# The first unit of an up projection made as plain products, with a written order for VectorE and ACT around it

## The chip, the cores and the metric

One core of one Trainium2 chip runs the whole block. The metric is the device time of one execution in microseconds (us), the median of repeated runs. The engines are TensorE (PE: matmuls, and PEld, its weight loads), VectorE (DVE), ScalarE (ACT), GpSimd (POOL) and SyncE (SP), which here issues the transfers between memory and the on-chip arrays. TensorE accumulates in banks of PSUM; all else lies in SBUF.

## What is computed

A decoder block on 1024 tokens of width 1024, in float32:

```python
h = rms_norm(x, mix_norm_g)
proj = h @ w_in
...
x = x + merged @ w_out
h2 = rms_norm(x, ffn_norm_g)
up = h2 @ w_up                      # 1024 x 5632
a, val = up[..., :D_FF], up[..., D_FF:]      # D_FF = 2816
a = causal_depthwise_conv(a, conv_w, conv_b) # 3 taps over tokens
x = x + (gelu(a) * val) @ w_down
return rms_norm(x, final_norm_g)
```

The case is about the end of `merged @ w_out` and the start of `h2 @ w_up`.

## The kernel before

**Arithmetic.** Each float32 operand of a matmul is split in a high part (a rounded copy, made on ACT, L161) and a low part (the rest, a subtraction, L162, on VectorE or POOL); this is `to_parts`. A product of two operands takes three matmuls, high·high, high·low and low·high (`PASSES`).

**Products.** Large products are made by a scheme of seven products in place of eight (Strassen-Winograd). The left matrix is quartered (A11, A12, A21, A22; first index the half of the tokens, second the half of the inner dimension), and the seven products P1 to P7 take as left operands A11, A12, A22 and the sums S1, S2, S3, S4; the right operands are sums of quarters of the weights. A product of the up projection has 4 steps of the inner dimension with 3 matmuls each: 12 matmuls of a 128x128 weight with 512 tokens. P2 is added into the PSUM bank of P1, P4 into that of P7, P3 into that of P5, so a product that reopens a bank must wait until the bank's first content has been read out.

**Up projection.** 22 units. Unit `ff` is 128 columns of the gate and 128 columns of the value, for both halves of the tokens (four results of 128x512). `up_op` (with `weight_op`, L253 to L276) makes the weight operands, `up_product` issues the matmuls (L1566) and what reads their banks: P1's bank is copied by ACT (`t1`, L1579), after P2 it is the gate of the first half of the tokens, which goes through `convolve` (an Identity with bias on ACT, L1523, two shifted multiply-adds on VectorE, L1525, with the two columns at the edge of the halves kept in `edge`, then a Gelu on ACT, L1532); `u2 = t1 + P6`, `v = u2 + P7` (L1587), and so on to the second gate `c21` and the two values; POOL multiplies gates and values (L1595, L1599); SP stores them in DRAM (`gd`). The list `order` sets in which order PE takes the products: the first two units, and P1 and P2 of the third, are interleaved, then each unit takes P1 and P2 of the next between its own products. `up_ahead` issues loads of weights up to nine places, operands up to four places ahead. P1's and P2's operands lie in rows 12 to 15 of the array `R`, the others in a pool of four buffers. For unit 0 VectorE stands in for POOL (`free`).

**Left operands.** `left_parts` splits a left matrix into 4 high and 4 low parts of 128x512. Rows of arrays are fixed (A11, A12 in `G0`, A22, S2 in `G1`, S3, S1, S4 in `R`).

**Output projection.** Its seven products run in the order P1, P2, P6, P5, P3, P7, P4 (L1454), each over four blocks of 128 tokens and four steps. When P3 (blocks 0 to 3) or P4 (blocks 4 to 7) of a block is read out (L1447), the block is complete: ACT squares it (`square_h`, L1411), POOL makes the scale (`finish_rms`, L1788 to L1793), ACT and VectorE scale one half each (`xn`, L1420 and L1421), PE transposes it (`turn_h`, `ht`, L1368), VectorE multiplies the gain in (L1372), and for the blocks 4 to 7 `sums` (L215 to L220) makes the sources of S1 to S4 out of two blocks. `after` and `tick` put a step a few matmuls further on.

**Order.** PE runs in the order of the program. The order of VectorE, ACT and POOL is set by a scheduler that places each instruction by its own estimates; each engine then works its list strictly in order and waits where an input or a buffer is not there yet.

Of the kernel before, what the change touches and what calls it, by code (L numbers as in the profile page):

```python
# [11 lines left out]
F32 = mybir.dt.float32  # L12
# [8 lines left out]
P = 128  # L21
# [72 lines left out]
def block_kernel(  # L94
# [115 lines left out]

    def sums(rows_of, raw, s3, b, eng):

        a11, a12 = raw[:, b - 4, lower], raw[:, b - 4, upper]
        a21, a22 = raw[:, b, lower], raw[:, b, upper]
        eng.tensor_tensor(s3[:, b - 4, :], a11, a21, ALU.subtract)  # L215
        nc.vector.tensor_tensor(a21, a21, a22, ALU.add)  # L216
        nc.vector.tensor_tensor(a11, a21, a11, ALU.subtract)
        if b == NB - 1:
            left_parts(rows_of, "S2", raw[:, 0:4], 0)
        nc.vector.tensor_tensor(a12, a12, a11, ALU.subtract)  # L220
# [1037 lines left out]
    def out_op(s):  # L1258

        if s < 3:  # L1260
            t = two(lead, s)
        elif (s - 3) % 8 < 4:
            t = two(R, 12 + (s - 3) % 8)
        else:
            t = wq.tile([P, 2, HALF], F32R, name=f"op_wo_{s}", tag="op", bufs=4)
# [43 lines left out]
    UP_ROWS = MIX_ROWS  # L1309
# [15 lines left out]

    def up_op(ff, name):
        if name in ("P1", "P2"):
            counts["up_op"] += 1
            row = 12 + counts["up_op"] % 4
            op = R[:, row, :].rearrange("p (a k c) -> p a k c", a=2, k=QK)  # L1330
        else:
            op = wq.tile([P, 2, QK, P], F32R, name=f"op_{name}_{ff}", tag="op", bufs=4)
        free = nc.vector if ff == 0 else nc.gpsimd
# [17 lines left out]
    def up_ahead(i, far, look):  # L1351

        while ready["load"] < min(i + far, len(order)):
# [4 lines left out]
        while ready["op"] < min(i + look, len(order)):  # L1358
            up_op(*order[ready["op"]])
            ready["op"] += 1  # L1360

    GAIN = 8 + NCT + 4 * NFF

    def turn_h(b, xn):
        for c in range(2):
            pt = (acc_tile if out_raw else tr_tile)(f"ht_{b}_{c}")
# [14 lines left out]
        if b >= 4:  # L1381
            sums(UP_ROWS, Y, s3, b, nc.vector)

# [31 lines left out]
    def finish_h(b):  # L1415

        nc.sync.dma_start(x1_t[:, b, :], Y[:, b, :])
        rs = finish_rms(nc, small, mhalf, sqs2[b], f"n2_{b}")
        xn = [temp(f"xn_{b}_{c}") for c in range(2)]
# [513 lines left out]
```

## Time and profile before

| | us |
|---|---|
| median of 3 runs | 1430.82 (1429.61 to 1431.01) |
| profiled execution | 1429.11 |
| its span | 1427.4 |
| PE busy in the span | 1388.0 (97%) |
| VectorE / ACT / POOL busy | 1016.4 / 650.6 / 313.7 |

The times of single instructions are from the profiled execution, counted from the start of its span. The difference of 1.7 us between the profiled execution's time and its span lies around the span. An instruction's row has its start, its duration, engine, line, the result and the operands, and in brackets how long the engine had been idle ahead of it and what it waited for.

### The profile page before, as it was taken

To read this page: it belongs to the slowest core of one execution; us is meant where nothing else is said; L and a number is where in the kernel's file an instruction comes from. 1 tells how busy PE (TensorE), PEld (TensorE's weight loads), DVE (VectorE), ACT (ScalarE), POOL (GpSimd) and SP (SyncE) were. 2 spreads that over 40 slices of the span, in tenths; PEclk is the share of its full clock that TensorE was granted. 3 is DMA by queue.
4 is the path that set the end of the run, shared out by engine and by line. 5 is a ranking of instruction groups with operands and counts; after the bars stand their busy time and mean duration, and the time that the engine had idled before them with its cause. 6 is when DMAs were issued, how large, how long until landed. Compare 5 with 4: busy or idle time off the path is not lost. (4 is left out here: it accounts for less than half of the span.)

```text
span 1427.4 us, 19350 instructions
## 1 busy us (share of the span) xinstructions
PE 1388.0 (97%) x6522; PEld 1145.4 (80%) x6522; DVE 1016.4 (71%) x1888; ACT 650.6 (46%) x1266; POOL 313.7 (22%) x303
## 2 busy tenths in 40 slices
PE   8899999999999999999998799999999999999997
PEld 7777788888888788887886588888888887888886
DVE  7877677676886987768878866665666557676674
ACT  5554255555553333534455433433333435354453
POOL 0002000000231000111001555556655544000002
PEclk9999999999999999999999999999999999999999
DMA  6013635354435996793731222223333226987663
GB/s 238 15 49 104 193 88 182 97 171 134 137 113 189 332 309 232 230 301 119 265 133 59 82 103 76 91 92 118 118 118 109 90 97 229 379 307 242 198 208 118
DMA packets 140338, 230.71 MB, mean 162 GB/s; under 512 B 13392, under 2 KB 57168, under 8 KB 140240
## 3 DMA queue, kind: packets, MB, share of 16 engines
q1 hardware_dynamic: 138800, 227.33, 47.7%
q10 hardware_dynamic: 1440, 2.16, 0.4%
q8 instruction: 51, 0.84, 0.2%
q14 instruction: 47, 0.39, 0.1%
HBM read 163.57 MB, written 64.29 MB: 160 GB/s over the span
## 5 line engine op out<-in xcount | busy, mean ns | idle before, releaser
L477 PE MATMUL in_P<-R,G 128*128 128x512 f32 x1008 | 243.8, 394 | 0.0
L477 PEld LDWEIGHTS in_P<-R,G 128*128 128x128 f32 x1008 | 185.7, 188 | 36.8
L1688 PE MATMUL dn<-R 128*128 128x512 f32 x924 | 209.6, 389 | 0.0
L1688 PEld LDWEIGHTS dn<-R 128*128 128x128 f32 x924 | 173.5, 188 | 36.0
L1566 PE MATMUL uP<-R,op_P 128*128 128x512 f32 x792 | 191.4, 395 | 0.0
L1566 PEld LDWEIGHTS uP<-R,op_P 128*128 128x128 f32 x792 | 149.6, 189 | 34.9
L161 ACT ACTIVATE G<-wr 128x512 fp32r<-128x512 f32 x126 | 79.1, 629 | 152.0 <-PE in_P L477 114.7
L1566 PE MATMUL uP<-G,op_P 128*128 128x512 f32 x528 | 133.2, 401 | 11.9 <-DVE Y L1587 7.8
L1566 PEld LDWEIGHTS uP<-G,op_P 128*128 128x128 f32 x528 | 100.6, 192 | 37.7 <-issue 7.0
L1566 PE MATMUL up<-G,R 128*128 128x512 f32 x528 | 127.6, 391 | 1.7 <-ACT t L1579 1.7
L477 PE MATMUL in_P<-G,G 128*128 128x512 f32 x504 | 123.2, 395 | 1.5 <-DVE C L504 1.5
L1566 PEld LDWEIGHTS up<-G,R 128*128 128x128 f32 x528 | 99.0, 188 | 23.2 <-ACT t L1579 2.1
L477 PEld LDWEIGHTS in_P<-G,G 128*128 128x128 f32 x504 | 92.7, 188 | 20.8 <-issue 1.3
L162 DVE TENSOR_TENSOR G<-wr,G 128x512 fp32r<-128x512 f32 x126 | 88.0, 699 | 22.1 <-ACT G L161 22.0
L161 ACT ACTIVATE op_P<-up 128x512 fp32r<-128x512 f32 x88 | 55.1, 628 | 100.7 <-DVE up L264 58.9
L161 ACT ACTIVATE R<-db 128x512 fp32r<-128x512 f32 x77 | 48.3, 628 | 68.1 <-PE dn L1688 53.5
L162 DVE TENSOR_TENSOR R<-db,R 128x512 fp32r<-128x512 f32 x77 | 52.8, 689 | 28.1 <-ACT R L161 27.8
L1595 POOL TENSOR_TENSOR Y<-Y 128x512 f32<-128x512 f32 x22 | 35.0, 1592 | 138.4 <-ACT Y L1532 138.4
L870 POOL TENSOR_TENSOR ld<-ld,w 128x256 f32<-128x256 f32 x16 | 11.2, 719 | 236.7 <-DVE w L858 236.7
L477 PE MATMUL in_P<-G 128*128 128x512 f32 x252 | 62.1, 393 | 0.0
L162 POOL TENSOR_TENSOR op_P<-up,op_P 128x512 fp32r<-128x512 f32 x42 | 59.3, 1411 | 2.5 <-ACT op_P L161 2.5
L162 POOL TENSOR_TENSOR wbl<-wbs,wbh 128x512 fp32r<-128x512 f32 x12 | 16.4, 1378 | 196.0 <-DMA gated<-C 139.9
(265 smaller groups left out, 2478.9 us busy)
## 6 DMA issues: line engine op xcount, KB each, us to landing
wr<-in_w_in_dram SPq DMA_DIRECT2D x46, 512.0 KB, 4.0
up<-in_w_up_dram SPq DMA_DIRECT2D x44, 512.0 KB, 4.1
dA<-gd SPq DMA_DIRECT2D x55, 256.0 KB, 5.1
wd<-in_w_down_dram SPq DMA_DIRECT2D x44, 256.0 KB, 5.3
wT<-wd SPq DMA_DIRECT2D x44, 256.0 KB, 3.3
gd<-Y SPq DMA_DIRECT2D x44, 256.0 KB, 2.0
dS<-gS SPq DMA_DIRECT2D x44, 256.0 KB, 4.2
db<-wT SPq DMA_DIRECT2D x44, 256.0 KB, 4.7
```

The lines of the kernel that those rows point to most:

```text
L161: nc.scalar.activation(hi, src, AF.Copy)
L162: lo_eng.tensor_tensor(lo, src, f32(hi), ALU.subtract)
L477: nc.tensor.matmul(acc, op[:, w, kt, :], left[LEFT[name], kt][:, a, :], start=opened and kt == 0 and i == 0, stop=kt == QK - 1 and i == 2, ...
L870: nc.gpsimd.tensor_tensor(v4(o[:, 0:256]), v4(o[:, 0:256]), wb(g), ALU.mult)
L1566: nc.tensor.matmul(acc, op[:, w, kt, :], left[LEFT[name], kt][:, a, :], start=opened and kt == 0 and i == 0, stop=kt == QK - 1 and i == 2, ...
L1595: nc.gpsimd.tensor_tensor(ge1, ge1, v, ALU.mult)
L1688: nc.tensor.matmul(accs[blk], dops[s][:, 0, a, blk * P : (blk + 1) * P], dops[s][:, 1, w, :], start=SEQ[j] not in CONTINUES and kt == 0 an ...
```

## The change

1. Unit 0 of the up projection is made without the seven products: `plain_product_up` makes the gate of the first half of the tokens (`gate0`), its value (`value0`), the gate of the second half (`gate1`) and its value (`value1`), each 24 matmuls (8 steps, 3 passes). It takes the plain quarters A11, A12 for the first half and A21, A22 for the second, and four operands of unsummed weights (`plain_up_op`), made while the output projection's P4 runs and used by both halves. A21's parts are new and lie in the rows that S4 takes later.
2. From the start of the output projection's P4 until unit 1's P3 the order on VectorE and ACT is that of the program (`manual_schedule`), written out in the last loop of the output projection and in `beginning_up`. `sums` is replaced by `sums_h`, and the left operands S2, S3, S1, S4 are split at the places that are written there.
3. The list `order` begins with P1, P2 of unit 1, P1, P2 of unit 2 (between `value0` and `gate1`), then the other five products of unit 1; from unit 2 on it is as before. VectorE stands in for POOL in unit 1.
4. The pool of four operand buffers becomes one tile `opx` of four rows, with fixed rows for the first operands.

```diff
-        free = nc.vector if ff == 0 else nc.gpsimd
+        free = nc.vector if ff == 1 else nc.gpsimd
...
-    order = [(0, "P1"), (1, "P1"), (0, "P2"), (2, "P1"), (1, "P2"), (2, "P2"), (0, "P6"), (1, "P6")]
-    order += [(0, "P7"), (0, "P5"), (0, "P4"), (0, "P3")]
-    order += [(1, "P7"), (1, "P5"), (1, "P4"), (1, "P3")]
+    order = [(1, "P1"), (1, "P2"), (2, "P1"), (2, "P2")]
+    order += [(1, name) for name in ("P6", "P7", "P5", "P4", "P3")]
...
+        if name == "P4":
+            first_up.enter_context(
+                tc.manual_schedule(engines={mybir.EngineType.DVE, mybir.EngineType.Activation})
+            )
         for n in range(4):
             s = 4 * j + n
             for m in range(4):
+                if name == "P4" and n >= 2 and m == 2:
+                    turn_h(2 + n, acc_tile)
...
             if name == "P4":
-                up_ahead(0, 4, n)
+                plain_up_op(n // 2, n % 2)
+                if n:
+                    scale_h(3 + n)
+                up_ahead(5, 0)
...
+        for n in range(KT):
+            k, kt = n // QK, n % QK
+            for i, (w, a) in enumerate(PASSES):
+                nc.tensor.matmul(
+                    acc, plain_up[which, k][:, w, kt, :], left[f"A{h + 1}{k + 1}", kt][:, a, :],
+                    start=n == 0 and i == 0,
+                    stop=n == KT - 1 and i == 2,
+                )
...
+    def beginning_up():
+        tt = nc.vector.tensor_tensor
+        gate0 = plain_product_up(0, 0, {
+            1: [lambda: turn_h(6, tr_tile), lambda: up_ahead(7, 1)],
+            5: [lambda: scale_h(7), lambda: up_ahead(7, 2), lambda: turn_h(7, tr_tile)],
+        })
+        left_parts(UP_ROWS, "A21", Y[:, 4:8], 0)
+        keep_edge(0, gate0)
+        taps(ge_of(0, 0), gate0, 0, None)
+        value0 = plain_product_up(0, 1, {})
+        left_parts(UP_ROWS, "A22", Y[:, 4:8], 1)
+        nc.scalar.activation(ge_of(0, 0), ge_of(0, 0), AF.Gelu)
+        up_ahead(7, 3)
+        tt(ge_of(0, 0), ge_of(0, 0), value0, ALU.mult)
+        store_g(0, 0, ge_of(0, 0))
+        up_product(1, "P1")
+        for b in (4, 5):
+            sums_h(b)
+        up_ahead(7, 4)
+        up_product(1, "P2")
+        for b in (6, 7):
+            sums_h(b)
+        up_product(2, "P1")
+        left_parts(UP_ROWS, "S2", Y[:, 0:4], 0)
+        up_product(2, "P2")
+        for b in range(4):
+            tt(Y[:, b, upper], Y[:, b, upper], Y[:, b, lower], ALU.subtract)
+        for ff in (1, 2):
+            keep_edge(ff, banks[ff, "P2"])
+            taps(ge_of(ff, 0), banks[ff, "P2"], ff, None)
+        up_ahead(9, 5)
+        for ff in (1, 2):
+            nc.scalar.activation(ge_of(ff, 0), ge_of(ff, 0), AF.Gelu)
+        gate1 = plain_product_up(1, 0, {})
+        left_parts(UP_ROWS, "S3", s3, 0)
+        up_ahead(9, 6)
+        taps(ge_of(0, 1), gate1, 0, edges.pop(0))
+        value1 = plain_product_up(1, 1, {})
+        left_parts(UP_ROWS, "S1", Y[:, 4:8], 0)
+        nc.scalar.activation(ge_of(0, 1), ge_of(0, 1), AF.Gelu)
+        up_ahead(9, 7)
+        tt(ge_of(0, 1), ge_of(0, 1), value1, ALU.mult)
+        store_g(0, 1, ge_of(0, 1))
+        up_product(1, "P6")
+        up_ahead(9, 8)
+        left_parts(UP_ROWS, "S4", Y[:, 0:4], 1)
```

How instructions move is shown at three places; a row has the line in its own version, the operation, result and operands. First ACT at the end of the output projection (`up_0_0` and `up_1_0` are unit 0's gate and value weights, `sq_b` and `xn_b_0` the square and the scaled half of block b). Before:

```order
L1411 ACTIVATE own_6227,sq_4_6645<-Y_5416 128x512
L1420 ACTIVATE xn_4_0_6755<-Y_5416,fr_n2_4_6753 128x512
L1411 ACTIVATE own_6227,sq_5_6691<-Y_5416 128x512
L1420 ACTIVATE xn_5_0_6781<-Y_5416,fr_n2_5_6779 128x512
L1411 ACTIVATE own_6227,sq_6_6709<-Y_5416 128x512
L1420 ACTIVATE xn_6_0_6823<-Y_5416,fr_n2_6_6821 128x512
L161 ACTIVATE R_75<-up_0_2_6759 128x512
L161 ACTIVATE R_75<-up_0_1_6733 128x512
L1411 ACTIVATE own_6227,sq_7_6727<-Y_5416 128x512
L1420 ACTIVATE xn_7_0_6865<-Y_5416,fr_n2_7_6863 128x512
```

The same place in the change:

```order
L1413 ACTIVATE own_6228,sq_5_6682<-Y_5416 128x512
L161 ACTIVATE R_75<-up_0_0_6686 128x512
L1426 ACTIVATE xn_4_0_6776<-Y_5416,fr_n2_4_6744 128x512
L1413 ACTIVATE own_6228,sq_6_6703<-Y_5416 128x512
L161 ACTIVATE R_75<-up_1_0_6688 128x512
L1426 ACTIVATE xn_5_0_6814<-Y_5416,fr_n2_5_6772 128x512
L1413 ACTIVATE own_6228,sq_7_6720<-Y_5416 128x512
L161 ACTIVATE opx_6148<-up_1_0_6688 128x512
L1426 ACTIVATE xn_6_0_6852<-Y_5416,fr_n2_6_6810 128x512
L161 ACTIVATE opx_6148<-up_0_1_6748 128x512
L1426 ACTIVATE xn_7_0_6889<-Y_5416,fr_n2_7_6848 128x512
```

Between a block's square and its scaling there now stand the next block's square and a high part of a weight.

Second, VectorE on its way to unit 1's add to v (`L1587` before, `L1632` in the change, the row with uP7_1). Before:

```order
L1525 SCALAR_TENSOR_TENSOR Y_5416<-Y_5416,chan_80 128x511
L1529 SCALAR_TENSOR_TENSOR Y_5416<-edge_0_6963,chan_80,Y_5416 128x1
L1525 SCALAR_TENSOR_TENSOR Y_5416<-Y_5416,chan_80 128x510
L1529 SCALAR_TENSOR_TENSOR Y_5416<-edge_0_6963,chan_80,Y_5416 128x2
L1598 TENSOR_TENSOR Y_5416<-Y_5416,uP5_0_7128 128x512
L1547 TENSOR_TENSOR own_6227<-Y_5416 128x512
L1587 TENSOR_TENSOR Y_5416<-Y_5416,uP7_1_7188 128x512
```

In the change (the two groups of four are low parts of S1 and of S4):

```order
L162 TENSOR_TENSOR R_75<-Y_5416,R_75 128x512 x4
L162 TENSOR_TENSOR opx_6148<-up_1_1_6752,opx_6148 128x512
L1751 TENSOR_TENSOR own_6228<-own_6228,pu_1_1_7102 128x512
L1630 TENSOR_TENSOR Y_5416<-t1_1_6977,uP6_1_7140 128x512
L261 TENSOR_TENSOR up_0_1_6748<-up_0_1_6748 128x512
L162 TENSOR_TENSOR opx_6148<-up_0_1_6748,opx_6148 128x512
L162 TENSOR_TENSOR R_75<-Y_5416,R_75 128x512 x4
L162 TENSOR_TENSOR opx_6148<-up_1_1_6752,opx_6148 128x512
L1632 TENSOR_TENSOR Y_5416<-Y_5416,uP7_1_7171 128x512
```

The add to v of unit 1 now stands behind the low parts of S4, the last left operand; before it stood behind unit 0's second convolution.

An instruction from outside the written order can stand inside it, as a weight operand of unit 3 does on VectorE, between unit 0's block sums and the taps of units 1 and 2:

```order
L1578 COPY edge_1_7044<-up_1_6964 128x2
L162 TENSOR_TENSOR R_75<-up_0_3_7167,R_75 128x512
L1548 SCALAR_TENSOR_TENSOR Y_5416<-up_1_6964,chan_80,Y_5416 128x511
L1548 SCALAR_TENSOR_TENSOR Y_5416<-up_1_6964,chan_80,Y_5416 128x510
L1578 COPY edge_2_7049<-up_2_7005 128x2
```

It is the low part for (3,"P2"), into a row of `R` that gate1 reads.

Third, POOL at the first products of unit 2 (`t3_2` is the source of P7's operand). Before:

```order
L162 TENSOR_TENSOR op_P3_1_7185<-up_1_1_6873,op_P3_1_7185 128x512
L1595 TENSOR_TENSOR Y_5416<-Y_5416 128x512
L1599 TENSOR_TENSOR Y_5416<-Y_5416 128x512
L162 TENSOR_TENSOR op_P6_2_7204<-up_0_2_6759,op_P6_2_7204 128x512
L162 TENSOR_TENSOR R_75<-up_0_4_7268,R_75 128x512
L162 TENSOR_TENSOR op_P7_2_7250<-t3_2_7205,op_P7_2_7250 128x512
```

In the change:

```order
L261 TENSOR_TENSOR up_0_2_6750<-up_0_2_6750 128x512
L162 TENSOR_TENSOR opx_6148<-up_0_2_6750,opx_6148 128x512
L162 TENSOR_TENSOR R_75<-up_0_3_7167,R_75 128x512
L162 TENSOR_TENSOR R_75<-up_0_4_7250,R_75 128x512
L1640 TENSOR_TENSOR Y_5416<-Y_5416 128x512
L1644 TENSOR_TENSOR Y_5416<-Y_5416 128x512
L162 TENSOR_TENSOR opx_6148<-t3_2_7187,opx_6148 128x512
```

The two multiplications of unit 1 stand between the operands, and the low part for unit 2's P7 behind them.

More of the change, by code (lines that the diff above doesn't have):

```diff
@@ L1349, in block_kernel, with up_ahead @@
     ready = {"load": 0, "op": 0}
-    def up_ahead(i, far, look):
-        while ready["load"] < min(i + far, len(order)):
+    def up_ahead(loads, opened):
+        while ready["load"] < min(loads, len(order)):
             ff, name = order[ready["load"]]
@@ L1462, in block_kernel @@
     own = s3 = junk = None
+    first_up = ExitStack()
     for blk in range(4):
@@ L1552, in sums_g, with keep_edge, plain_product_up @@
         sums_load(ff + 2)
+    def keep_edge(ff, acc):
+        edges[ff] = small.tile([P, 2], F32, name=f"edge_{ff}", tag="edge")
+        nc.vector.tensor_copy(edges[ff], acc[:, HALF - 2 :])
+    def plain_product_up(h, which, beside):
+        name = f"pu_{h}_{which}"
+        if h or which:
+            acc = ps_d.tile([P, HALF], F32, name=name, tag="dn")
+        else:
+            acc = acc_tile(name)
+        for n in range(KT):
[6 more added lines that the diff above has]
+                )
+            for fn in beside.get(n, ()):
+                fn()
+        return acc
     def up_product(ff, name):
```

105 lines of the change are left out of this document (61 added, 44 removed).

## The prediction

> **What bounds the kernel now.** I read the page's busy shares first: PE is busy for 97% of the span, so a change must move PE's work or PE's waits. Then the windows. The columns are the stretch and its length, then busy time (and instructions) of PE, its weight loads, VectorE (DVE), ACT and POOL, then the granted clock of PE, the DMA share and GB/s.
>
> ```profile
> span 1427.4 us, 19350 instructions
> 748.00:824.44 76.44, 62.03 (x265) 48.14 (x265) 65.44 (x103) 37.62 (x69) 25.53 (x25) 0.96 0.19 66
> 824.44:1185.00 360.56, 360.56 (x1561) 293.84 (x1560) 219.74 (x332) 135.81 (x219) 202.92 (x149) 1.00 0.30 104
> ```
>
> The first stretch holds the end of the output projection's P4 and the first two units of the up projection. PE idles there for 76.44 − 62.03 = 14.4 us, and VectorE is busy for 65.44 of 76.44. From (2,"P6") at 824.44 on PE has no idle time at all for 360 us. So whatever (2,"P6") and the few products behind it gain or lose against before goes to the end unchanged. What to work out is when these products start.
>
> The waits of PE in this stretch, grouped (engine, result, line, releaser: us, times, longest), and PE's own timeline (start, us, line, idle time before and its releaser):
>
> ```profile
> PE uP L1566 <- DVE Y L1587: 6.3, 2, 4.7
> PE uP L1566 <- ACT op_P L161: 2.5, 2, 1.3
> PE up L1566 <- ACT t L1579: 1.7, 1, 1.7
> PE ht L1368 <- DVE Y L1447: 1.4, 1, 1.4
> PE ht L1368 <- ACT R L161: 1.0, 1, 1.0
> ...
> 751.78 2.24 PE L1454 MATMUL wo_P<-op_wo,G 128*128 128x512 f32 x9
> 759.03 3.01 PE L1566 MATMUL up<-G,R 128*128 128x512 f32 x12
> 763.84 0.66 PE L1368 MATMUL ht<-ident,xn 128*128 128x128 f32 x4 [1.36 <-DVE Y L1447]
> 803.35 5.45 PE L1566 MATMUL uP<-G,op_P 128*128 128x512 f32 x12 [4.73 <-DVE Y L1587]
> 818.79 3.02 PE L1566 MATMUL uP<-G,op_P 128*128 128x512 f32 x12 [1.59 <-DVE Y L1587]
> 821.65 2.96 PE L1566 MATMUL uP<-R,op_P 128*128 128x512 f32 x12
> 824.44 2.96 PE L1566 MATMUL uP<-G,op_P 128*128 128x512 f32 x12
> 827.24 2.94 PE L1566 MATMUL up<-G,R 128*128 128x512 f32 x12
> 830.01 4.35 PE L1566 MATMUL uP<-R,op_P 128*128 128x512 f32 x18
> ```
>
> The largest idle time is that ahead of the product that reopens a unit's P7 bank (P4 in the program, unit 0 at 803.35, unit 1 at 818.79), and VectorE's add at L1587, which empties that bank, ends it. VectorE's queue sets this stretch. A product of 12 matmuls takes 824.44 − 821.65 = 2.79 us of PE.
>
> **The change, part by part.** All times below are on before's clock; the first 748 us are the same program.
>
> *PE's work.* Unit 0 was 7 products of 12, now it is 4 of 24: +12 matmuls, **+2.79 us**. Only a loss of idle time can pay for it: 14.4 us were there.
>
> *The end of the output projection.* Rows of the norm in before:
>
> ```profile
> 749.26 0.69 DVE L1447 TENSOR_TENSOR Y<-Y,wo_P 128x512 f32<-128x512 f32 x1
> 750.04 0.63 ACT L1411 ACTIVATE own<-Y 128x512 bf16<-128x512 f32 x1 [0.92 <-DVE Y L1447]
> 752.08 0.72 ACT L1420 ACTIVATE xn<-Y,fr_n 128x512 f32<-128x512 f32 x1 [1.31 <-POOL fr_n L1793]
> 741.39 4.26 ACT L161 ACTIVATE G<-Y 128x512 fp32r<-128x512 f32 x8
> 772.70 0.68 DVE L1372 TENSOR_TENSOR Y<-ht,chan 128x512 f32<-128x512 f32 x1
> 742.04 4.91 DVE L162 TENSOR_TENSOR G<-Y,G 128x512 fp32r<-128x512 f32 x8 [0.17 <-ACT G L161]
> ```
>
> A block's scaling starts 752.08 − 750.04 = 2.04 us behind its square. In the fixed order ACT makes the next block's square and a high part of a gate weight between the two (0.63 + 4.26/8 = 0.53 us), and this high part waits until VectorE's turn has come round; by my walk each of the scalings of blocks 4, 5 and 6 starts some 1.6 us later than PE's three steps of P4 (about 2.8 us each) allow. The transposes now stand inside P4's last block and the first plain product, where PE takes them in order: 3 × 1.6 = **+4.7 us** of waits, where before had 1.36 + 0.97 at its transposes. Two of the waits lie ahead of the first plain product, which starts near 762.3 instead of 759.03, the third inside it. Bounds: 0 if ACT gets through in PE's time, 4.7 if none is hidden; I take the upper end, since the rows of one block already add up to more than one step of PE. Against it, block 7 now comes without other work ahead of it: its last gain (L1372 at 772.70) ends near 770.9.
>
> *VectorE's queue.* VectorE's operation on 128x512 costs 4.91/8 = 0.60 us in a queue (0.64 with its tail), ACT's high part 0.53. From the end of gate0 (762.3 + 5.6 for 24 matmuls + 3.3 for the transposes of blocks 6 and 7, of which 1.6 is the third wait = 771.2) to unit 1's add to v, VectorE has 32 low parts of left operands (19.2 us), 12 block sums (8.2), 4 subtractions (2.4), the weight sums and low parts of units 1 and 2 (3.2), two products with value (1.2), three convolutions' taps with their edges (6.3), u2 and v (1.2): about 41 us. Onto this come round trips, in which VectorE or its partner waits because the order is fixed:
>
> ```profile
> 759.37 0.69 DVE L216 TENSOR_TENSOR Y<-Y 128x512 f32<-128x512 f32 x1
> 760.09 0.69 DVE L217 TENSOR_TENSOR Y<-Y 128x512 f32<-128x512 f32 x1
> 780.17 0.77 ACT L1523 ACTIVATE Y<-up,chan 128x512 f32<-128x512 f32 x1
> 781.25 0.75 DVE L1525 SCALAR_TENSOR_TENSOR Y<-up,chan,Y 128x511 f32<-128x511 f32 x1
> 783.56 1.28 ACT L1532 ACT_TABLE_LOAD   x1
> 784.86 0.63 ACT L1532 ACTIVATE Y<-Y 128x512 f32<-128x512 f32 x1
> ```
>
> VectorE goes 0.72 us from one result to the next that needs it. Each "Identity" of a convolution (0.77) holds up the taps behind it, each table load (1.28) the high parts behind it, and so the low parts on VectorE. I count eight such places at 0.7 to 1.0 us: edge to Identity 0.9, table load 0.7, S2's first high part 0.8, a low part of (3,"P2") placed inside the fixed stretch, which waits until gate1's last reading of its row, 1.0, gate1's Identity 0.9, P6's high part 0.7, S3 behind two Gelus 1.0, P4's high part 0.8: about **7 us**, between 0 (all covered) and 10. VectorE reaches the end of v at 771.2 + 41 + 7 = 819.4.
>
> ```profile
> 817.97 0.67 DVE L1587 TENSOR_TENSOR Y<-Y,uP 128x512 f32<-128x512 f32 x1
> ```
>
> Before, unit 1's v ended at 818.64. So the product behind it, (1,"P4"), starts at 819.7 against 818.79, and (2,"P6") two products later at 825.35 against 824.44: **+0.9 us**. The four plain products, +2.79 us of PE and the waits of P4 are thus mostly paid by before's own idle time, since VectorE needs nearly as long as it did. On the way PE waits by my walk for 0.9 twice (P2 behind P1 of the same unit needs the bank that ACT's 0.57 copy empties), 2.8 ahead of (1,"P6"), 3.1 ahead of (1,"P7"), 1.0 ahead of (1,"P5") and 3.4 ahead of (1,"P4").
>
> *POOL's tail.* POOL ran these in before:
>
> ```profile
> 813.72 1.29 POOL L1595 TENSOR_TENSOR Y<-Y 128x512 f32<-128x512 f32 x1
> 800.28 3.45 POOL L162 TENSOR_TENSOR op_P<-t,op_P 128x512 fp32r<-128x512 f32 x1 [9.89 <-DVE op_P L162]
> 788.68 1.71 POOL L162 TENSOR_TENSOR op_P<-up,op_P 128x512 fp32r<-128x512 f32 x1
> ```
>
> An operation costs 1.29 alone, up to 1.71 beside VectorE, once 3.45. Now the low part for (2,"P7") stands seventh in a row: a weight sum, P6's low part, two of the plain-read rows of units 3 and 4, unit 1's two products, then it. They start when ACT and VectorE are out of the fixed stretch, near 822.2; at about 1.45 each the seventh ends at 832.3. (2,"P7") started at 830.01 before, with its low part long there. It now starts at 832.3: **+2.3 us**, which takes in the +0.9. Between 1.29 and 1.71 each this is 831.2 to 834.2, +1.2 to +4.2. I keep the middle, as half of these have VectorE beside them. Behind (2,"P7") PE is gapless again in before, and I find nothing that gives the time back.
>
> What unit 0 loses (4 weight sums, 3 of its 7 weight operands, its u2 and v) came off VectorE and ACT; unit 1's sum for P7, its P4 sum and low parts come onto VectorE in their place, since the engine that stands in for POOL is now chosen for unit 1. The 41 us counts what is left, so no term of its own stands for it. The transfers cost nothing by my sum:
>
> ```profile
> up<-in_w_up_dram SPq DMA_DIRECT2D x44, 512.0 KB, 4.1
> ```
>
> Unit 0's two loads go out in P7, half a product and more ahead of P4, and SP's queue has 66 GB/s to move in this stretch; P4's 16 small steps cover the 4.1 us of a landing. With that cover gone the first high part, and all of ACT behind it, would be up to 4.1 late.
>
> **The sum.** The profiled execution took 1429.11 (span 1427.4 + 1.7 around it), 1.7 under the median of 1430.82. 1429.1 + 2.3 = 1431.4 there; **1430.82 + 2.3 = 1433.1** against the median. 0.2%, about what a measurement can tell from no change, is 2.9 us.
>
> **Rivals.**
>
> *The clock falls ahead of (1,"P4").* In before, a wait of 4.73 us halved PE's clock:
>
> ```profile
> 798.00:803.00 5.00, 0.62 (x3) 0.18 (x1) 5.00 (x9) 2.19 (x4) 2.71 (x1) 0.88 0.36 100
> 803.30:808.60 5.30, 5.25 (x12) 4.18 (x13) 4.28 (x5) 1.15 (x2) 3.77 (x4) 0.50 0.36 104
> ```
>
> The product at 803.35 took 5.45 us against 3.02 for the same product at 818.79: 2.4 us lost. A mean of 0.88 over five us is 0.6 us lost, or the last 1.2 us at half clock; so it fell near 801.8, and the wait had begun at 803.35 − 4.73 = 798.6. A wait past about 3.2 us is in danger; mine are 2.8, 3.1 and 3.4. If one halves the clock behind it, and VectorE does not hide it, the time is 1433.1 + 2.4 = **1435.5**. For it: three waits near the edge. Against it: the waits of 1.59 and less kept the clock. By the Trainium skill (TensorE: Matmul & The Clock Gate, "What's actually happening") the clock drops after at least one idle window of some 3.4 us, and the window runs freely. By that rule my 3.4 would be cut in some runs and not in others; the row above agrees in size.
>
> *The fixed order hides what I charge.* If ACT's high parts of gate weights fit into the gaps at the transposes, the 4.7 us is gone; if gate1's round trips (the low part of (3,"P2") 1.0, Identity 0.9, Gelus 1.0, P6 0.7) are covered by PE's value1, 3.6 more. VectorE's queue, and POOL's row behind it, would come up to 8.3 earlier: 1430.82 + 2.3 − 8.3 = **1424.8**, or with half of it about 1429. For it: before had waits of only 1.36 and 0.97 at its transposes. Against it: VectorE's 41 us of work alone, from 771, end at 812.
>
> *POOL falls behind.* If one or two of the seven take 3.45, as one did in before, (2,"P7") starts 2 to 4 us later still: **1435 to 1437**. For it: VectorE's additions run beside every one of them. Against it: 3.45 came once.
>
> *The change does not do what it says*: some operation from outside stands in the fixed stretch (one does, charged above at 1.0). More of them would be slower by as much each.
>
> **Chances.** Forecast 0.42; its own range is 1431 to 1435 (within 0.2% 0.26, slower 0.16). Clock 0.20 (slower 0.18, within 0.02). Hidden round trips 0.22 (faster 0.18, within 0.04). POOL 0.10 (slower). Others 0.06 (faster 0.03, within 0.02, slower 0.01). Together faster 0.21, within 0.2% 0.34, slower 0.45. The range takes in most of the gaining case and the clock's: 1425.5 to 1437.0.
>
> **What would show it.** The first plain product starts some 3 us later than 759.03, with waits of 1 to 2 us at the transposes of blocks 4 to 6 released by ACT's xn; no wait of 4.7 us anywhere; v of unit 1 ends 0 to 2 us later than 818.64; (2,"P7") is released by POOL's low part; PE gapless behind it. The forecast is wrong if VectorE has idle time of over 10 us between 771 and 819, if PE's clock row falls under 0.9 anywhere there, or if (2,"P7") waits for nothing.

## The result and the profile after

| | median | runs |
|---|---|---|
| before | 1430.05 us (1426.97 to 1433.7) | 20 |
| changed | 1432.24 us (1429.54 to 1435.07) | 20 |

The ratio is 1.0016, 95% interval 1.0007 to 1.0025: slower by 2.2 us, clear of noise, and less than 0.2%. By the interval it lies between 1.0 and 3.6 us. The profiled execution of the changed kernel is the longest of its 20:

```profile
span 1433.3 us, 19415 instructions
```

It took 1435.07 us, 6.0 more than the profiled execution of before. Part of that lies ahead of the change. PE enters the output projection after a wait for VectorE; the row of before, then that of the changed kernel:

```profile
677.47 7.24 PE L1454 MATMUL wo_P<-lead,G 128*128 128x512 f32 x30 [1.76 <-DVE g L1285]
```

```profile
677.50 9.89 PE L1461 MATMUL wo_P<-lead,G 128*128 128x512 f32 x30 [2.91 <-DVE g L1274]
```

Both start at the same time; the 30 matmuls take 2.65 us longer in the second, at a lower clock (0.70 against 1.00). In the fourteen profiles of this study the output projection's P4 begins between 742.39 and 748.91 us, though the kernels do the same work up to there. So all places below are counted from P4's first matmul, which is at 746.20 in before and at 748.91 in the changed kernel, 2.71 later. The stretch runs from there to the start of unit 3's P2. From its end to the end of the execution the fourteen profiles differ by 0.5 us only (593.2 to 593.7 us), so executions differ by their stretch and by what lies ahead of it. The stretch in before and then in the changed kernel (length, then busy time of PE, its weight loads, VectorE, ACT, POOL; clock; DMA):

```profile
746.20:835.60 89.40, 74.99 (x321) 58.67 (x320) 73.44 (x114) 42.03 (x76) 33.66 (x31) 0.96 0.22 77
```

```profile
748.91:841.80 92.89, 78.72 (x333) 61.14 (x332) 70.87 (x113) 41.96 (x77) 20.58 (x23) 0.96 0.21 72
```

The stretch grew by 3.5 us in these two profiles. PE has its 12 more matmuls, and its idle time is 14.2 us against 14.4: the change moved the idle time and did not remove it. PE's waits in the changed kernel's stretch, and then its timeline at them:

```profile
PE ht L1372 <- ACT xn L1426: 4.0, 3, 1.4
PE uP L1611 <- DVE Y L1632: 3.2, 1, 3.2
PE uP L1611 <- ACT opx L161: 2.4, 1, 2.4
PE uP L1611 <- DVE own L1552: 1.6, 1, 1.6
PE up L1611 <- ACT t L1624: 1.4, 2, 0.7
PE uP L1611 <- POOL opx L162: 0.9, 1, 0.9
PE uP L1611 <- DVE own L1751: 0.7, 1, 0.7
```

```profile
757.38 1.23 PE L1372 MATMUL ht<-ident,xn 128*128 128x128 f32 x8 [1.35 <-ACT xn L1426]
...
765.20 1.55 PE L1590 MATMUL pu<-G,R 128*128 128x512 f32 x6
...
806.16 4.63 PE L1611 MATMUL uP<-G,opx 128*128 128x512 f32 x12 [2.37 <-ACT opx L161]
812.39 3.03 PE L1611 MATMUL uP<-R,opx 128*128 128x512 f32 x12 [1.61 <-DVE own L1552]
...
822.39 4.58 PE L1611 MATMUL uP<-G,opx 128*128 128x512 f32 x12 [3.22 <-DVE Y L1632]
...
829.60 2.94 PE L1611 MATMUL uP<-G,opx 128*128 128x512 f32 x12
...
836.58 5.38 PE L1611 MATMUL uP<-R,opx 128*128 128x512 f32 x22 [0.85 <-POOL opx L162]
```

The waits at the transposes (757.38 is the first of three), the waits for VectorE ahead of unit 1's products, the lower clock behind two of them (4.63 and 4.58 us where 3.03 is the usual), and the wait for POOL at unit 2's P7, which has made two of its 12 matmuls by then, are all there. (Here and below (1,P4) is the product P4 of unit 1, (2,P7) the product P7 of unit 2.)

### The profile page after: what moved, and what is told of

Read it like the earlier page. It is cut to its first block, busy times and chain, and to the rows that moved or that the text cites. A ratio compares the mean times of both kernels' runs of the same rounds, so it can differ in the third digit from the quotient of the medians.

```text
span 1433.3 us, 19415 instructions
## 1 busy us (share of the span) xinstructions
PE 1393.8 (97%) x6534; PEld 1150.7 (80%) x6534; DVE 1010.1 (70%) x1887; ACT 650.7 (45%) x1266; POOL 301.4 (21%) x296
## 4 chain that ended last, share of the span: by engine, by line
PE 80%; DVE 8%; issue 4%; POOL 3%; DMA 2%; ACT 2%; SPq 0%; POOLq 0%; DVEq 0%; ACTq 0%
PE in_P L466 23%; PE uP L1611 18%; PE dn L1794 12%; PE up L1611 8%; PE wo_P L1461 5%; PE pa L1177 3%; PE pl L527 2%; PE pu L808 1%; DMA ld<-scr 1%; PE pu L1590 1%; PE pb L1177 1%; DVE R L162 1%; PE warm L319 1%; POOL st L860 1%; PE pm L617 1%
## 5 line engine op out<-in xcount | busy, mean ns | idle before, releaser
L1611 PE MATMUL uP<-R,opx 128*128 128x512 f32 x756 | 183.4, 396 | 3.2 <-DVE own L1552 1.6
L1611 PEld LDWEIGHTS uP<-R,opx 128*128 128x128 f32 x756 | 142.5, 189 | 37.4 <-ACT R L161 2.0
L161 ACT ACTIVATE G<-wr 128x512 fp32r<-128x512 f32 x126 | 79.1, 629 | 150.5 <-PE in_P L466 118.3
L1611 PE MATMUL uP<-G,opx 128*128 128x512 f32 x504 | 127.3, 403 | 6.8 <-DVE Y L1632 4.4
L1611 PEld LDWEIGHTS uP<-G,opx 128*128 128x128 f32 x504 | 96.9, 193 | 30.6 <-issue 5.2
L161 ACT ACTIVATE opx<-up 128x512 fp32r<-128x512 f32 x88 | 55.6, 631 | 132.6 <-DVE up L253 60.5
L1611 PE MATMUL up<-G,R 128*128 128x512 f32 x468 | 113.0, 391 | 0.7 <-ACT t L1624 0.7
L1611 PEld LDWEIGHTS up<-G,R 128*128 128x128 f32 x468 | 87.9, 188 | 19.9 <-ACT t L1624 1.1
L162 POOL TENSOR_TENSOR opx<-up,opx 128x512 fp32r<-128x512 f32 x40 | 56.6, 1415 | 0.0
```

The source lines that it names most:

```text
L161: nc.scalar.activation(hi, src, AF.Copy)
L162: lo_eng.tensor_tensor(lo, src, f32(hi), ALU.subtract)
L1611: nc.tensor.matmul(acc, op[:, w, kt, :], left[LEFT[name], kt][:, a, :], start=opened and kt == 0 and i == 0, stop=kt == QK - 1 and i == 2, ...
```

## The experiments

Each ratio stands against runs of before on the same chip; the medians of before were 1429.0 to 1429.7 us there, and 1430.05 beside the changed kernel. So a difference between a median below and the changed kernel's 1432.24 can be off by up to 1 us. "Stretch" is the time from P4's first matmul to unit 3's P2 in the profile.

| run | median us | ratio to before (95%) | stretch us |
|---|---|---|---|
| changed kernel | 1432.24 | 1.0016 (1.0007 to 1.0025) | 92.89 |
| e1 scalings first | 1427.98 | 0.9989 (0.9980 to 0.9998) | 89.87 |
| e2 v ahead of S4 | 1431.53 | 1.0012 (1.0000 to 1.0024) | 92.57 |
| e3 P7's low part on VectorE | 1430.62 | 1.0005 (0.9996 to 1.0014) | 91.80 |
| e4 free order | 1414.62 | 0.9893 (0.9877 to 0.9909) | 75.74 |
| f1 written order to gate0 only | 1420.16 | 0.9925 (0.9906 to 0.9945) | 79.77 |
| f2 written order from gate0 only | 1426.43 | 0.9981 (0.9968 to 0.9994) | 88.40 |
| f3 clock kept up | 1432.23 | 1.0013 (1.0001 to 1.0025) | 94.26 |
| f4 free order, P1s first | 1413.20 | 0.9876 (0.9856 to 0.9895) | 74.07 |
| g1 order mended | 1427.99 | 0.9989 (0.9974 to 1.0005) | 89.08 |
| g2 order rewritten | 1425.65 | 0.9977 (0.9963 to 0.9991) | 88.01 |
| g3 rewritten again | 1422.82 | 0.9951 (0.9934 to 0.9968) | 83.58 |
| g4 copy first | 1423.23 | 0.9962 (0.9947 to 0.9977) | 84.47 |

**e1: the scalings ahead of the next block's add.**

```diff
             elif name != "P1":
+                if name == "P4" and n:
+                    scale_h(3 + n)
                 out_result(name, n, accs[n])
...
                 plain_up_op(n // 2, n % 2)
-                if n:
-                    scale_h(3 + n)
```

> The scalings of blocks 4, 5 and 6 are put ahead of the next block's add and square on VectorE and ACT, and of the weight's high part; nothing else moves. In the changed kernel's profile PE waits 3 times 1.35 us for ACT's scaled half at the transposes. Theory (VectorE's queue, started by gate0's end, sets the stage): the three waits fall to under 0.3 us each, the first plain product starts 2.7 us earlier counted from P4's start, unit 1's add to v and (2,P6) come about 4 us earlier, and the median falls by 3 to 4 us against the changed kernel, to about 1428 to 1429.5, some 1 to 2 us under the kernel before. Rival (another wait ends last, VectorE's or ACT's later round trips or POOL's tail): the waits go and PE idles as much more ahead of (1,P6) to (1,P4); the median stays within 1 us of 1432.2.

It took 1427.98 us, 4.3 under the changed kernel, and the stretch is 3.0 shorter. The three waits of 1.35 became three of 0.3 to 0.5 (1.2 in all), and the wait ahead of (1,P4) came 2.8 us earlier, as VectorE's queue did. The theory holds. What is left is a longer wait ahead of unit 1's P7 and P5, with the clock down behind it, and a new wait at POOL:

```profile
804.39 8.63 PE L1611 MATMUL uP<-R,opx 128*128 128x512 f32 x24 [2.93 <-DVE own L1552]
814.38 3.03 PE L1611 MATMUL uP<-G,opx 128*128 128x512 f32 x12 [1.36 <-DVE Y L1632]
...
828.38 5.39 PE L1611 MATMUL uP<-R,opx 128*128 128x512 f32 x22 [2.19 <-POOL opx L162]
```

The clock stayed up behind the wait ahead of (1,P4), which gave 1.5 us, and (2,P7) then waited 1.3 longer for POOL. That the clock fell one place earlier cost nothing further down, since (1,P4) still waited for VectorE's queue.

**e2: S4's parts behind the add to v.**

```diff
-        left_parts(UP_ROWS, "S4", Y[:, 0:4], 1)
...
+        if (ff, name) == (1, "P7"):
+            left_parts(UP_ROWS, "S4", Y[:, 0:4], 1)
```

> S4's parts are split behind unit 1's P7 and its add to v instead of ahead of them; S4 is read by P3, the unit's last product. In the changed kernel's profile (1,P4) waits 3.22 us for this add and then runs at a lower clock (4.58 us for 12 matmuls against 3.03). Theory: the wait falls to about 1.2 us, the clock stays up, (2,P6) comes 2 us earlier by the wait and 1.5 more by the clock; the convolution behind P4 and with it the multiplication on POOL and the low part of (2,P7) come as much earlier, so that the median falls by 2 to 3.5 us, to 1428.5 to 1430. Rival (S4's parts are then late for (1,P3), which waits instead): no more than 0.5 us of gain. Rival (POOL's seven operations set (2,P7) by their own time): (2,P6) earlier, but (2,P7) waits 3 us for POOL, no gain in the median.

```profile
814.44 3.02 PE L1611 MATMUL uP<-G,opx 128*128 128x512 f32 x12 [0.26 <-DVE Y L1632]
819.38 4.58 PE L1611 MATMUL uP<-R,opx 128*128 128x512 f32 x12 [1.91 <-DVE Y L1636]
```

The wait ahead of P4 is nearly gone, and P3 behind it waits 1.9 us for the next reading of a bank, v plus P5, which now stands behind S4's parts, and the clock falls there instead. (It also falls ahead of that, behind a wait of 2.92 us at unit 1's P7 and P5: 24 matmuls in 7.32 us.) The first rival was right: the wait moved by one product. The median is 0.7 us under the changed kernel, which these runs cannot tell from none.

**e3: the low part for (2,P7) on VectorE.**

```diff
-        lo_eng = nc.vector if name in ("P2", "P5", "P4") or (ff < 3 and name == "P1") else free
+        lo_eng = nc.vector if name in ("P2", "P5", "P4") or (ff < 3 and name in ("P1", "P7")) else free
```

> The low part for (2,P7) is made on VectorE instead of POOL; nothing else is asked for. In the changed kernel's profile (2,P7) waits 0.85 us for POOL's low part, which stands behind unit 1's two multiplications. Theory of the prediction (POOL's tail costs 1.4 of the 2.3 us): the wait goes and the gain is 0.9 to 1.4 us. Rival (the low part is late only when PE comes early; VectorE is as late since it stands behind unit 1's second convolution): the wait becomes one for VectorE, gain 0 to 0.5 us. A median within 0.8 us of 1432.2 cannot be told from none, so the wait ahead of (2,P7) in the profile decides.

(2,P7) waits for nothing, and the stretch is 1.1 us shorter, as the theory said; the median is 1.6 under the changed kernel, with intervals that overlap. The tail on POOL is real, and about 1 us.

**e4: the same program in the scheduler's order.**

```diff
         if name == "P4":
-            first_up.enter_context(
-                tc.manual_schedule(engines={mybir.EngineType.DVE, mybir.EngineType.Activation})
-            )
+            pass
```

> The plain products stay, the written order of VectorE and ACT goes: the scheduler orders them as before the change. Theory (the 12 more matmuls and the new place of the four blocks' transposes and left operands cost what the written order then partly gives back): slower than the changed kernel by 2 to 8 us, 1434 to 1440, with waits at the left operands S2, S3, S1. Rival (the written order itself is the loss, by its round trips): faster than the changed kernel by 2 to 4 us.

1414.62 us: 17.6 under the changed kernel and, by the ratio, 1.07% under before. Both expectations were wrong in size and the theory in sign. PE's waits in its stretch, then the stretch, and VectorE's time from the last gain (L1376) to the end of unit 1's add to v:

```profile
PE up L1609 <- ACT t L1622: 1.9, 2, 1.2
PE ht L1372 <- ACT xn L1426: 0.2, 1, 0.2
```

```profile
745.28:821.02 75.74, 73.67 (x333) 59.43 (x332) 66.91 (x113) 41.40 (x76) 21.99 (x23) 1.00 0.25 82
766.26:802.67 36.41, 34.50 (x149) 27.54 (x148) 36.19 (x65) 23.84 (x42) 4.31 (x1) 1.00 0.08 25
```

The same from the last gain to v in the changed kernel:

```profile
773.78:822.24 48.46, 39.34 (x159) 30.11 (x157) 41.47 (x70) 24.29 (x43) 0.09 (x1) 0.96 0.06 22
```

VectorE (third busy time) works 36.2 of 36.4 us in the free order and 41.5 of 48.5 in the written one. Of the 12 us between them 7 are idle time, and 5 are work: in the free order three of the four subtractions for S3 and two more of the weights' low parts are done before the last gain ends, a low part for unit 3 comes after v, and two operations that need each other's result seldom follow each other (0.60 from start to start, not 0.72). VectorE's waits in the changed kernel, from the output projection's P4 to v, show where the idle time is:

```profile
DVE R L162 <- ACT R L161: 6.1, 5, 1.4
DVE opx L162 <- ACT opx L161: 3.4, 4, 1.4
...
DVE Y L1548 <- ACT Y L1546: 0.8, 1, 0.8
DVE own L1548 <- ACT own L1546: 0.8, 1, 0.8
...
DVE G L162 <- ACT G L161: 0.7, 1, 0.7
```

Ten times a low part waits for ACT's high part, which the program mostly makes just ahead of it, and twice a convolution's taps wait for ACT. Four of these waits, 1.37 us each, lie ahead of the last gain; the other eight, 6.4 us, are nearly all of the 7 us. In the free order VectorE waits for ACT for 0.2 us in all, from the output projection's P4 to v.

**f1 and f2: the written order in one half only.** In f1 it ends ahead of A21's parts, in f2 it begins there.

```diff
+        first_up.close()
         left_parts(UP_ROWS, "A21", Y[:, 4:8], 0)
```

> The written order of VectorE and ACT ends behind gate0's transposes, ahead of A21's parts; from there the scheduler orders them. In the free order's profile VectorE goes from the last gain to unit 1's add to v in 36.4 us without idle time, in the changed kernel's in 48.4: 6.5 us of idle time, 1.3 us since an operation there reads the one just before it (0.72 instead of 0.60 us), 4.2 us of work that the free order does earlier or later. Theory (most of the written order's price lies behind gate0): 8 to 12 us faster than the changed kernel, 1420 to 1424. Rival (the price is the late start: with the norm of the last blocks and the weights late, the rest follows): 0 to 4 us faster.

```diff
+        first_up.enter_context(
+            tc.manual_schedule(engines={mybir.EngineType.DVE, mybir.EngineType.Activation})
+        )
         left_parts(UP_ROWS, "A21", Y[:, 4:8], 0)
```

> The other half: the output projection's P4 and gate0 in the scheduler's order, the written order from A21's parts to unit 1's P3. Theory: the 4 us of waits at the transposes go, as when the scalings came first, and little else: 3 to 6 us faster than the changed kernel, 1426 to 1429. Rival: 8 us or more faster, as the weights' operands are ready and the rest has slack.

f1 is 12.1 us under the changed kernel, f2 5.8; together 17.9, where the whole order was worth 17.6 (by the ratios 1.26% and 1.23%). Both theories hold, and the two halves add up. In f1 PE keeps the waits at the transposes and has none of the others, but for the copy of P1's bank:

```profile
PE ht L1372 <- ACT xn L1426: 4.0, 3, 1.4
...
PE up L1611 <- ACT t L1624: 1.4, 2, 0.7
```

In f2 the transposes wait 0.3 us in all, and the waits ahead of unit 1's products and for POOL are those of e1.

**f3: PE kept at work in two waits.**

```diff
+        if (ff, name) in ((1, "P6"), (1, "P4")):
+            idle = tr_tile(f"idle_{name}")
+            for _ in range(8):
+                nc.tensor.matmul(idle, left["A11", 0][:, 0, :P], left["A11", 0][:, 0, :], start=True, stop=True)
```

> The changed kernel with 8 more matmuls of 128x512, whose result is not read, ahead of unit 1's P6 and 8 ahead of its P4, where PE waits 2.4 and 3.2 us. Theory (the clock that falls there costs 1.5 us behind P4 only, since VectorE hides it behind P6): both products at 3.0 us instead of 4.6, (2,P6) 1.5 us earlier counted from P4's start, median 0.5 to 1.5 us under 1432.2. Rival (the later waits absorb it): no change.

```profile
808.03 7.37 PE L1615 MATMUL uP<-R,opx 128*128 128x512 f32 x24 [2.93 <-DVE own L1552]
...
818.02 3.02 PE L1615 MATMUL uP<-G,opx 128*128 128x512 f32 x12 [0.81 <-DVE Y L1636]
...
823.67 2.96 PE L1615 MATMUL uP<-G,opx 128*128 128x512 f32 x12
...
832.02 6.93 PE L1615 MATMUL uP<-R,opx 128*128 128x512 f32 x22 [2.15 <-POOL opx L162]
```

(1,P4) takes 3.02 us instead of 4.58, and (2,P6) starts 79.1 us behind P4's start instead of 80.7: the clock's price is there as expected. The clock is not kept up throughout, though: it falls between the two places, at P7 and P5 of unit 1 (24 matmuls in 7.37 us), without moving (1,P4)'s start. And (2,P7) waits 2.15 for POOL instead of 0.85, goes on 0.2 us earlier only, and then runs at the lower clock itself (6.93 against 5.38), so that the stretch of this profile is 1.4 us longer than the changed kernel's. The median is the same. The rival was right: the later wait absorbs it.

**f4: free order, P1 of units 1 and 2 ahead of their P2.**

```diff
-    order = [(1, "P1"), (1, "P2"), (2, "P1"), (2, "P2")]
+    order = [(1, "P1"), (2, "P1"), (1, "P2"), (2, "P2")]
```

> The free order, and P1 of units 1 and 2 ahead of P2 of both, as in the kernel before. In the free order's profile PE waits 1.2 and 0.7 us for ACT's copy of P1's bank ahead of P2, the only waits left between P4 and unit 2. Theory: both go, 1.5 to 1.9 us under 1414.6. Rival (VectorE, without idle time there, is the bound and PE waits later for it): no change.

The program of `beginning_up` follows this order. Both waits for ACT's copy are gone, a stretch of 74.07 us against 75.74, which agrees with the theory. The median of 1413.20 is 1.4 under e4's; with four runs each that is not settled, but the version is the fastest here, 1.24% under before by the ratio.

**g1: four places of the written order mended.** e1's edit, e3's edit, S4's parts behind unit 1's P5, and the rows 14 and 15 exchanged, so that the row of (3,P2)'s operand is read by value1 and no longer by gate1.

```diff
-    plain_rows = {(0, 0): (R, 13), (0, 1): (R, 14), (1, 0): (R, 15), (1, 1): (opx, 0)}
+    plain_rows = {(0, 0): (R, 13), (0, 1): (R, 15), (1, 0): (R, 14), (1, 1): (opx, 0)}
...
-        left_parts(UP_ROWS, "S4", Y[:, 0:4], 1)
...
+        if (ff, name) == (1, "P5"):
+            left_parts(UP_ROWS, "S4", Y[:, 0:4], 1)
```

> The changed kernel, written order throughout, mended at four places: the scalings first, S4's parts behind unit 1's P5, the low part for (2,P7) on VectorE, and an operand row for (3,P2) that is read later. Theory (each place has its own price: 3.0 us at the transposes, 2.2 at POOL's low part, which showed once the transposes' waits were gone, about 1 at the row, 0 to 1.5 at S4): 1423 to 1426. Rival (a mended place only shows the next wait of the same queue): 1427 to 1429, as the scalings alone.

1427.99, what e1 alone gave: the rival. (1,P4) and (2,P7) wait for nothing, the waits ahead of unit 1's P6 and P7 stay (2.65 and 2.93 us), and P3 now waits for S4's parts, one by one; the first:

```profile
819.34 0.97 PE L1611 MATMUL uP<-R,opx 128*128 128x512 f32 x3 [0.74 <-DVE R L162]
```

**g2, g3, g4: the list rewritten.** g2 changes the order behind gate0 along these lines (`part_hi` and `part_lo` are the two halves of `left_parts`; g1's edits stand):

```diff
-        left_parts(UP_ROWS, "A21", Y[:, 4:8], 0)
-        keep_edge(0, gate0)
-        taps(ge_of(0, 0), gate0, 0, None)
-        value0 = plain_product_up(0, 1, {})
-        left_parts(UP_ROWS, "A22", Y[:, 4:8], 1)
+        part_hi("A21", low, 0)
+        part_lo("A21", low, 0)
+        keep_edge(0, gate0)
+        part_hi("A22", low, 1)
+        part_lo("A22", low, 1)
+        taps(ge_of(0, 0), gate0, 0, None)
+        part_hi("S3", s3, 0)
+        value0 = plain_product_up(0, 1, {})
+        sums_h((4, 5))
...
         up_product(1, "P2")
+        part_hi("S2", top, 0)
+        part_hi("S1", low, 0)
         up_product(2, "P1")
```

> Written order throughout, rewritten behind gate0 so that no operation of VectorE waits for ACT or reads the one just before it: the subtractions for S3 right behind each block's gain, other work between an edge and its convolution, high parts of S3 and S1 ahead of their low parts, sums in pairs. The place in the program and the operations are the same as in the changed kernel. Theory (the price is VectorE's idle time and late work in this one list, 12 us behind gate0 and 4 ahead of it, not that a list is written): 1414 to 1420. Rival (the fixed list holds up ACT or what comes after it in some other way): over 1422.

1425.65, the rival. PE's waits ahead of (1,P6), (1,P7) and (1,P4) are gone, and other places wait: ACT's copy of unit 2's P1 stands behind S1's four high parts, and S4's four low parts take 5.79 us beside POOL.

```profile
786.46 4.61 PE L1613 MATMUL up<-G,R 128*128 128x512 f32 x12 [2.60 <-ACT t L1626]
```

```profile
812.83 5.79 DVE L162 TENSOR_TENSOR R<-Y,R 128x512 fp32r<-128x512 f32 x4 [0.68 <-ACT R L161]
```

g3 moves S1's high parts behind the convolution of unit 2's first gate, that of unit 1 ahead of unit 2's edge, the subtractions for S3 behind block 7's scaling, and S4's parts back:

```diff
+        keep_edge(1, banks[1, "P2"])
+        part_lo("S3", s3, 0, (0, 1))
+        taps(ge_of(1, 0), banks[1, "P2"], 1, None)
+        up_ahead(9, 5)
+        keep_edge(2, banks[2, "P2"])
+        part_lo("S3", s3, 0, (2, 3))
+        taps(ge_of(2, 0), banks[2, "P2"], 2, None)
+        part_hi("S1", low, 0)
```

> The rewritten list of the run before, with the waits that its profile showed taken up: the copy of unit 2's P1 no longer behind S1's high parts (2.6 us and a lower clock behind it), unit 1's convolution ahead of unit 2's edge (VectorE was idle for 4.6 us), the subtractions for S3 behind block 7's scaling (2.1 us at its transposes), S4's parts ahead of unit 1's add to v again (four took 5.8 us instead of 2.5 beside POOL, and P3 waited for each). Theory (a written list costs what its waits cost): 1414 to 1419. Rival (each mended place shows the next): 1421 to 1425.

1422.82, 9.4 under the changed kernel, and inside the rival's range. One large wait is left:

```profile
778.70 8.02 PE L1611 MATMUL up<-G,opx 128*128 128x512 f32 x24 [4.19 <-ACT t L1624]
```

It is ACT's copy of unit 1's P1, behind a table load (1.28), a Gelu and a high part. g4 puts the copy first:

```diff
+        up_product(1, "P1")
         nc.scalar.activation(ge_of(0, 0), ge_of(0, 0), AF.Gelu)
         tt(ge_of(0, 0), ge_of(0, 0), value0, ALU.mult)
         store_g(0, 0, ge_of(0, 0))
-        up_ahead(7, 3)
-        up_product(1, "P1")
```

> The rewritten list once more, with ACT's copy of unit 1's P1 ahead of the first gate's table load, Gelu and unit 2's high part; nothing else. In the profile of the run before PE waits 4.19 us for this copy and then takes 8.0 us for 24 matmuls instead of 5.85, the largest of 7.7 us of waits between P4 and unit 2's P6. Theory (a written list costs what its waits cost): 3 to 5.5 us under 1422.8, 1417 to 1420, near the free order's 1414.6. Rival (the wait moves to unit 1's P2 or unit 2's products, whose operands are then later on ACT): 1421 to 1423.

```profile
775.89 6.19 PE L1611 MATMUL up<-G,opx 128*128 128x512 f32 x24 [1.19 <-ACT t L1624]
785.19 3.04 PE L1611 MATMUL up<-G,R 128*128 128x512 f32 x12 [3.11 <-ACT t L1624]
...
810.33 4.59 PE L1611 MATMUL uP<-G,opx 128*128 128x512 f32 x12 [2.77 <-DVE Y L1632]
```

1423.23: no gain. PE waits 3.0 us less for the copy, and 2.4 us more for the next copy and 1.8 more for the add to v. The rival again.

## Why the prediction was right, and what it left out

It forecast 2.3 us, and 2.2 were measured; within 0.2% and to the slower side. That they agree to 0.1 us is in part luck: in the profiles the stretch grew by 3.5 us. Of these 0.9 are VectorE's queue, as forecast, 1.5 the lower clock at (1,P4), which the sum left out, and 1.0 the wait for POOL, where 1.4 were forecast. Counted on before's clock (the profile's times less 2.71):

| step | predicted | measured |
|---|---|---|
| waits at the transposes | 4.7 | 4.0 |
| first plain product starts | 762.3 | 762.5 |
| A21's low parts start | 771.2 | 771.2 |
| VectorE from there to v: work, idle | 41, 7 | 41.5, 7.0 |
| unit 1's add to v ends | 819.4 | 819.5 |
| (1,P4) starts | 819.7 | 819.7 |
| (2,P6) starts | 825.35 | 826.9 |
| POOL's low part for (2,P7) ends | 832.3 | 833.8 |
| (2,P7) goes on behind it | 832.3 | 833.9 |

*PE's 12 matmuls and the transposes.* Right in size. e1 shows that the transposes' waits go to the end: without them the stretch is 3.0 us shorter.

*VectorE's queue sets (1,P4).* Right to 0.2 us in place, and right in idle time. The work of 41 us is right by luck: the step counts 32 low parts of left operands (19.2 us), but the six operands A21, A22, S2, S3, S1 and S4 have 24, which were busy for 15.0 us; and it has 3.2 us for the weights' sums and low parts, where four sums and eight low parts (one of them unit 3's) were busy for 8.4. The two errors nearly cancel. Its terms as they stand add up to 41.7.

*The clock.* It was given as a rival, at 0.20, and in the profiled execution it happened, behind a wait of 2.37 and one of 3.22 us. The granted clock was 0.63 over (1,P6), from 806.20 to 810.80, so one of the prediction's own signs of being wrong, a clock under 0.9 between 771 and 819, came true. At (1,P6) VectorE hid it: in f3 (1,P6) took 3.31 us, and (1,P4) starts at the same place. Its term of 2.4 was too large: (1,P4) took 1.5 longer, and f3 shows that taking this away gives nothing, since POOL's low part for (2,P7) is then waited for instead, and the clock falls behind that wait.

*POOL's tail.* POOL's work was right (10.1 us for the seven operations), the time at which they end was 1.5 us late, and the reason was not the one given. The step said that seven operations in a row, at about 1.45 us each from 822.2, end at 832.3. POOL's rows after:

```profile
824.31 1.29 POOL L261 TENSOR_TENSOR up<-up 128x512 f32<-128x512 f32 x1 [50.43 <-DVE up L253]
825.55 1.28 POOL L162 TENSOR_TENSOR opx<-up,opx 128x512 fp32r<-128x512 f32 x1
826.78 3.01 POOL L162 TENSOR_TENSOR R<-up,R 128x512 fp32r<-128x512 f32 x2
832.07 1.54 POOL L1640 TENSOR_TENSOR Y<-Y 128x512 f32<-128x512 f32 x1 [2.27 <-ACT Y L1543]
833.58 1.73 POOL L1644 TENSOR_TENSOR Y<-Y 128x512 f32<-128x512 f32 x1
835.27 1.26 POOL L162 TENSOR_TENSOR opx<-t,opx 128x512 fp32r<-128x512 f32 x1
```

POOL starts at 821.6 on before's clock, and stands idle for 2.27 us in the middle: the first of unit 1's multiplications waits for ACT's Gelu of unit 1's second convolution, which follows from (1,P4)'s end, and the low part stands behind it in POOL's order. What failed is that the seven run in a row: a chain of PE, VectorE and ACT sets the start of the fifth, and VectorE's operations, slowed beside POOL, made f3 gain so little. From the add ahead of the convolution to POOL's multiplication f3 took 5.75 us and the changed kernel 4.38. The tap over a single column makes 1.0 of the 1.4 us between them, with 1.24 us in f3 against 0.21; VectorE's two taps in f3, and then POOL's two low parts beside them:

```profile
822.98 1.78 DVE L1548 SCALAR_TENSOR_TENSOR Y<-Y,chan 128x511 f32<-128x511 f32 x1
824.68 1.24 DVE L1552 SCALAR_TENSOR_TENSOR Y<-edge,chan,Y 128x1 f32<-128x1 f32 x1
```

```profile
822.45 3.46 POOL L162 TENSOR_TENSOR R<-up,R 128x512 fp32r<-128x512 f32 x2
```

*The gaining rival* gave 0.22 to the round trips being hidden. They were not, and its argument against itself, "VectorE's 41 us of work alone, from 771, end at 812", stood for the written order only: with the order free, VectorE has 36.2 us of work from 766.3 and ends at 802.7.

*What the prediction did not ask* is what the two halves of the change are worth apart. It priced the list as written and found a small loss; it never set the plain products beside it in another order. e4 shows a gain and a loss that nearly cancel: the plain products with the new list of products, ordered by the scheduler, are 15.1 us faster than before in the difference of the medians (1.07% by the ratio), and the written order on top costs 17.6. The gain is PE's idle time: from 14.4 us in before's stretch to 2.1 in e4's, 12.3 us; its busy time is even 1.3 us shorter, with 12 matmuls more, in part since none runs at the lower clock, which cost before 2.4 us at 803.35. That the plain unit does it by needing no sums of blocks, so that PE has 96 matmuls to make while VectorE makes them, fits the profile and was not tried by itself; the new list of products and VectorE's standing in for POOL in unit 1 came with it.

The runs settle that the written order costs 17.6 us here, a third of it ahead of A21's parts (f2) and two thirds behind (f1). In g1 to g4 its cost shows as a row of waits: a place that is mended opens the next one. Whether a list written by hand can reach the free order is open: four rounds of rewriting gave 9 of the 17.6 us.

## What to carry to other kernels

When a change takes work away and fixes an order at the same time, price the two apart, and try the first without the second: here one is worth 15 us and the other costs 17.6, and together they look like a change of nothing. In a written order a low part right behind its high part, an add right behind the sum that it reads, or a copy behind another unit's table load each costs a round trip that a looser order fills; count VectorE's idle time against its work before moving single places, since a mended place shows the next wait of the same queue. A wait's price is only paid if the next wait down the path does not take it: follow it to the first place without slack.

## What the runs showed of the hardware

The clock fell after shorter waits than the 3.2 us that before's rows suggested: behind a wait of 1.91 us in e2 (12 matmuls in 4.58 us) and of 2.15 in f3 (22 in 6.93 against 5.38). The length of the wait does not decide it: the wait for POOL's low part of (2,P7) was as long in e1 (2.19) and in f2 (2.15), and the clock stayed up (22 matmuls in 5.39 and 5.38 us), and in g4 it stayed up behind a wait of 3.11 us (12 in 3.04). The row of f2:

```profile
825.88 5.38 PE L1609 MATMUL uP<-R,opx 128*128 128x512 f32 x22 [2.15 <-POOL opx L162]
```

By the Trainium skill (TensorE: Matmul & The Clock Gate, "What's actually happening") the clock drops after at least one idle window of some 3.4 us; in e2 it drops behind a wait of little over half of that, and the measurement decides. What decides between the waits of 2 to 3 us is not shown here.

VectorE is held up where POOL works on SBUF beside it: in g2 four low parts took 5.79 us while POOL made a sum and low parts of its own, where four take 2.49 to 2.50 in the changed kernel. The Trainium skill (SBUF — State Buffer, "SBUF: two separate sides") says that the two share a port pair as an exclusive lock, held for a whole instruction; the tap over one column that took 1.24 us in f3, against 0.21 in the changed kernel, agrees: it ends at 825.92, and POOL's two low parts at 825.91.
